# The last group of the second feed-forward product by eight block products, 128 tokens at a time, with its operands split during the seventh group

## The chip, the cores and the metric

The kernel runs on one core of one Trainium2 chip. The metric is the device time of one execution in microseconds, taken as the median of several runs. The core's engines are TensorE (PE in the profile), VectorE (DVE), ScalarE (ACT), GpSimd (POOL) and SyncE (SP), and DMA engines that move data beside them. Each of these engines works through its own list of instructions in the order in which the program issued them.

## The reference, cut to what matters

One decoder layer for 512 tokens of width 1024 in float32: a norm, three token mixers from one input projection, a gated merge, an output projection; then a feed-forward part and a final norm. The change touches only the feed-forward part's second product and the final norm behind it:

```python
h2 = rms_norm(x, g_ffn[l])
x = x + jnp.square(jax.nn.relu(h2 @ w_ff1[l])) @ w_ff2[l]
return rms_norm(x, g_final)
```

`w_ff1` is 1024x4096 and `w_ff2` 4096x1024. The hidden activation is therefore 512 tokens by 4096 columns.

## The kernel before, in words

**Split operands.** Each float32 operand of a matmul is split into a rounded part `hi` (a copy on ACT) and a rest `lo` (a subtraction on DVE that needs `hi`). One block of a product is three matmuls, hi by hi, hi by lo and lo by hi, in `mm3` (L96 to L100). In the feed-forward's second product the hidden activation is the stationary operand (128 columns of it, tokens) and 512 columns of the weight are streamed.

**Units and hooks.** The program is a list of units. A unit has a piece of matmul work and an eviction that is issued when the next unit begins. The main loop (L1082 to L1111) goes through the units. For unit i it issues, in this order: the `hi` copies of the weights due at slot i, the eviction of unit i-1, the `lo` subtractions of those weights, the hooks of slot i (table `pre`), a further weight load for each weight that was split, and then the matmuls of unit i. So what stands in the hooks of slot i goes to ACT, DVE and POOL while PE is in unit i-1 or at the start of unit i, and what it makes is for unit i or later.

**Two kinds of weight transfer.** Plain weight tiles come through SP into three `raw` buffers (L963) and are split at L971 (ACT) and L977 (DVE, shown as L79). A new load takes the buffer of the third load before it, so it waits for that one's `lo` subtraction. The second kind are block sums of `w_ff2`: POOL loads one 512 KB block (`w_load`, L748) and adds another to it by an accumulating transfer (`w_add`, L753); `w_split` (L757 to L762) splits the result into a ring of three `hi` and three `lo` buffers.

**The second product in groups of 512 hidden columns.** There are eight groups, g = 0 to 7. For one group the hidden tile is cut in 2x2 blocks (256 tokens by 256 hidden columns), the weight likewise (256 hidden columns by 512 outputs), and the 2x2 block product is done by seven block products of sums of blocks in place of eight of plain blocks. One such block product is 2 token tiles x 2 tiles of 128 hidden columns x 3 matmuls = 12 matmuls, so a group is 84. `form_11`, `form_12`, `form_22` split plain hidden blocks, `sum_3` and `sums` build sums of hidden blocks on DVE, and `form_s` splits these. The seven products are `stages` 1, 2, 5, 6, 3, 7, 4 (L778). `gather` (L773) adds each to the two or more quarters of the result `x2` that it belongs to; "B" is one accumulator that the products 1, 6, 7 and 4 add to in turn, and `gather` reads it between them.

**How groups overlap.** In the loop at L891, iteration g (1 to 7) has eight units: a tile of the first product of group g (24 matmuls, `f1_unit`, evicted by `ev_1`: DVE L691, ACT square L692), then products 1 and 2 of group g-1, a tile, products 5 and 6, a tile, products 3 and 7, a tile, product 4. The operands of the group's products are made in hooks during these. Iteration 8 (`last`) has no tiles of the first product left: seven units with one block product each, with its hooks (`sums`, `form_12`, three `w_split`, two `w_add`, `form_s` twice and more) squeezed into these seven slots.

**The end.** The final norm needs for each token the sum of squares over its 1024 outputs (`fin_sq`, ACT L807), a reciprocal root (`fin_rstd`: DVE, DVE L127, then a power on POOL) and a scaling by it and by the gain (`fin_dve` L822 on DVE, or `fin_gmul` and `fin_act` L827), and then the store. The table `ends` hangs these behind the products 2, 3 and 7 of the last group, and `fin_last` (L830) does the last two token tiles behind product 4.

Of the kernel before, what the change touches and what calls it, by code (L numbers as in the profile page):

```python
# [7 lines left out]
F32 = mybir.dt.float32  # L8
F32R = mybir.dt.float32r
# [27 lines left out]
def trunk_kernel(ctx: ExitStack, tc, xT, x_t, w_f, w_t, w_bc, w_a, w_o, w_1, w_2, vecs, rows, gfin, w_sg, cst, lmask, out):  # L37
# [31 lines left out]
    def hslot(i, dt):  # L69
        return rp.tile([P, 2 * S], dt, tag=f"h{i}", name=nm("h"))  # L70
# [31 lines left out]
    def cs(k, n=P):  # L102
        return slice(k * n, (k + 1) * n)
# [77 lines left out]
    def at(table, slot, fn, *a):  # L181
        table.setdefault(slot, []).append((fn, a))
# [561 lines left out]
    def w_tile(kind, dt):  # L744
        turns[kind] = turns[kind][1:] + turns[kind][:1]
        return zpair(turns[kind][-1], dt)

    def w_load(n, g, src, kind):  # L748
        if g < NG:
            wr[n, g] = w_tile(kind, F32)  # L750
            pool.dma_start(wr[n, g], w_2[g, src[0], src[1]])

    def w_add(n, g, src):  # L753
        if g < NG:
            pool.dma_start(wr[n, g], w_2[g, src[0], src[1]], accum_op=ALU.add)  # L755

    def w_split(n, src, g):  # L757
        if 0 <= g < NG:
            hi, lo = w_tile("h", F32R), w_tile("l", F32R)
            act.activation(hi, wr[src, g], AF.Copy)  # L760
            tt(dve, lo, wr[src, g], f(hi), ALU.subtract)
            wr[n, g, "r"] = (hi, lo)  # L762

    def product(g, a, b, key, start, stop):
        if start:
# [40 lines left out]
    def fin_sq(t, col):  # L806
        act.activation(tmp(), x2[t][:, cs(col, S)], AF.Square, accum_out=sf[col][:, t:t + 1])  # L807
# [22 lines left out]
    def fin_last():  # L830
        for j in range(2):
            t = 2 + j
            xv = x2[t][:, :S]
            tt(dve, xv, xv, part["B"][j], ALU.add)
            fin_sq(t, 0)
            fin_rstd(t, 1)
            fin_act(t, cs(1, S))
            fin_dve(t, cs(0, S))

    ends = {2: [(fin_sq, (0, 0)), (fin_sq, (1, 0))],  # L840
            3: [(fin_sq, (0, 1)), (fin_sq, (1, 1)), (fin_rstd, (0, 2))]
            + [(fin_dve, (t, cs(0, D))) for t in range(2)],
            7: [(fin_sq, (t, 1)) for t in (2, 3)] + [(fin_gmul, (t, 1, dve)) for t in (2, 3)]}

    o0 = len(units)
    for n in range(2):
        for j in range(4):
# [24 lines left out]

    W11, W12, W21, W22 = (0, 0), (0, 1), (1, 0), (1, 1)

    def chain(g):
        return f"c{g}"

    def early(u):

        at(pre, u, w_load, "c", 0, W12, "c")  # L880
# [7 lines left out]
    at(pre, f0 + 6, fin_gain)  # L888
    f1_unit(3)
    b0 = len(units)  # L890
    for g in range(1, NG + 1):  # L891
        u = len(units)
        last = g == NG
        h = g - 1
        if not last:
            order_ = [(4 * g, None), (None, (1, 2)), (4 * g + 1, None), (None, (5, 6)), (4 * g + 2, None), (None, (3, 7)),
                      (4 * g + 3, None), (None, (4,))]
            for i, ps in order_:
                if ps is None:
                    f1_unit(i, slot=len(units) - 1)  # L900
                else:
                    stage_unit(h, ps)
            sl = [u + x for x in range(8)]
        else:
# [10 lines left out]
        at(pre, sl[0], w_split, "21", "21", h)  # L915
# [15 lines left out]
        at(pre, sl[0], form_12)  # L931
        at(pre, sl[0], w_split, "t1", "c", h)
        at(pre, sl[0], w_add, "c", h, W22)
        at(pre, sl[0], form_s, "s12", 6)
        at(pre, sl[0], w_load, "22", h, W22, "p")
        at(pre, sl[1], form_s, "s34", 12)
        at(pre, sl[1], w_load, "11", g, W11, "p")
        at(pre, sl[2], w_split, "t3", "t3", h)
        at(pre, sl[2], w_split, "t2", "c", h)
        at(pre, sl[2], w_add, "c", h, W21)  # L940
        at(pre, sl[3], form_22)
        at(pre, sl[3], w_load, "t3", g, W12, "t3")
        at(pre, sl[4], w_split, "22", "22", h)
        at(pre, sl[4], sum_3)
        at(pre, sl[4], form_11)
        at(pre, sl[4], w_load, "c", g, W12, "c")
        at(pre, sl[5], w_split, "t4", "c", h)
        at(pre, sl[5], w_add, "t3", g, W22)
        at(pre, sl[5], w_load, "21", g, W21, "p")
        at(pre, sl[6], w_split, "11", "11", g)  # L950
        at(pre, sl[6], w_add, "c", g, W11)
        if g < NG - 1:
            at(pre, sl[7], sums)

    raws, ws = {}, {}
    order = [x for s in sorted(when) for x in when[s]]
# [210 lines left out]
```

## Time and profile before

| | |
|---|---|
| median of 3 runs | 850.81 us (849.37 to 851.62) |
| profiled execution: time, span | 851.69 us, 849.8 us |
| mean granted TensorE clock | 0.986 of full speed |
| PE busy | 823.8 us, 97% of the span |
| DVE, ACT, POOL busy | 65%, 41%, 19% |

The span runs from the first to the last instruction, and the execution's own time is 1.89 us above it. In a timeline a row is: start, duration, engine, line, operation, what it writes and reads, and in brackets how long the engine sat idle before it and what ended that. Matmul records overlap, since the engine is pipelined, so the step between starts, not the duration, is what one costs. A clock of 1.00 in a stretch is 2.4 GHz, one of 0.50 is 1.2 GHz.

### The profile page before, as it was taken

What the parts mean: (1) busy time and instruction counts of PE and PEld (TensorE: products, weight loads), DVE (VectorE), ACT (ScalarE), POOL (GpSimd) and SP (SyncE); (2) the same over time, 40 slices, a digit from 0 to 9 for tenths busy, and PEclk for the clock granted to TensorE, in tenths of its full rate; (3) what the DMA queues carried; (4) which work ended last, traced back from release to release, by engine and by line L of the source; (5) the groups of instructions that cost most, each with busy time, mean ns of one, the idle gap of its engine ahead of it and who ended that gap; (6) DMA issues with size and microseconds to landing.
All of it is one profiled execution on the core that took longest, in us unless ns stands there. A gap on an engine that the chain in (4) does not pass through costs nothing. (4 is left out here: it accounts for less than half of the span.)

```text
span 849.8 us, 9890 instructions
## 1 busy us (share of the span) xinstructions
PE 823.8 (97%) x3786; PEld 685.3 (81%) x3786; DVE 553.6 (65%) x720; ACT 350.9 (41%) x525; POOL 162.8 (19%) x193
## 2 busy tenths in 40 slices
PE   9999899999999999999999999999999999999973
PEld 7888688888888888888888888888888888888752
DVE  7556989978573445554444457595968686868574
ACT  7567355354333232232322445343435353534232
POOL 4313565661210000000000020102111111112000
PEclk9999999999999999999999999999999999999986
DMA  8321222212112323222234264837474656665432
GB/s 302 123 100 50 74 100 76 72 54 95 55 62 100 105 93 103 96 86 95 92 137 173 100 211 126 233 125 198 125 197 139 184 156 168 169 176 148 100 49 100
DMA packets 31296, 105.06 MB, mean 124 GB/s; under 512 B 3601, under 2 KB 3985, under 8 KB 31249
## 3 DMA queue, kind: packets, MB, share of 16 engines
q1 hardware_dynamic: 20448, 66.13, 21.9%
q0 software_dynamic: 10368, 37.75, 18.2%
q8 instruction: 29, 0.48, 0.2%
q10 hardware_dynamic: 432, 0.55, 0.2%
q14 instruction: 19, 0.15, 0.1%
HBM read 102.33 MB, written 2.10 MB: 123 GB/s over the span
## 5 line engine op out<-in xcount | busy, mean ns | idle before, releaser
L98 PE MATMUL acc<-x,wh 128*128 128x512 f32 x672 | 263.6, 392 | 0.0
L100 PE MATMUL acc<-x,wl 128*128 128x512 f32 x672 | 261.6, 389 | 0.0
L99 PE MATMUL acc<-x,wh 128*128 128x512 f32 x672 | 261.5, 389 | 0.0
L971 ACT ACTIVATE wh<-raw 128x1024 fp32r<-128x1024 f32 (+1 forms) x112 | 114.6, 1025 | 245.9 <-PE acc L99 143.5
L79 DVE TENSOR_TENSOR wl<-raw,wh 128x1024 fp32r<-128x1024 f32 (+1 forms) x118 | 150.1, 1273 | 43.9 <-ACT wh L971 43.8
L100 PEld LDWEIGHTS acc<-x,wl 128*128 128x128 f32 x672 | 126.1, 188 | 26.3
L98 PEld LDWEIGHTS acc<-x,wh 128*128 128x128 f32 x672 | 126.2, 188 | 25.9 <-issue 0.2
L99 PEld LDWEIGHTS acc<-x,wh 128*128 128x128 f32 x672 | 126.2, 188 | 25.6 <-issue 0.2
L79 DVE TENSOR_TENSOR z<-z,z 128x1024 fp32r<-128x1024 f32 x56 | 67.8, 1220 | 38.8 <-ACT z L760 38.8
L79 DVE TENSOR_TENSOR h<-h,acc 128x512 f32<-128x512 f32 x124 | 79.4, 682 | 11.0 <-PE acc L100 11.0
L98 PE MATMUL acc<-z,h 128*128 128x512 f32 x192 | 77.3, 403 | 7.8 <-DVE h L79 6.9
L760 ACT ACTIVATE z<-z 128x1024 fp32r<-128x1024 f32 x56 | 58.1, 1051 | 52.2 <-PE acc L100 28.1
L100 PE MATMUL acc<-z,h 128*128 128x512 f32 x192 | 77.0, 401 | 1.9 <-DVE h L79 1.9
L99 PE MATMUL acc<-z,h 128*128 128x512 f32 x192 | 77.1, 401 | 0.8 <-DVE z L79 0.8
L755 POOL DMA_DIRECT2D z<-w x32 | 28.1, 877 | 253.4 <-DVE z L79 208.4
L79 DVE TENSOR_TENSOR h<-h,h 128x256 f32<-128x256 f32 (+4 forms) x94 | 70.2, 752 | 7.0 <-ACT h L736 3.6
L692 ACT ACTIVATE h<-tmp 128x512 f32<-128x512 f32 x32 | 20.3, 633 | 126.9 <-DVE tmp L691 126.9
L79 DVE TENSOR_TENSOR tmp<-acc,rb 128x512 f32<-128x512 f32 x28 | 19.4, 691 | 79.0 <-PE acc L100 79.0
L79 POOL TENSOR_TENSOR tmp<-tmp,tmp 128x512 f32<-128x512 f32 x15 | 20.4, 1357 | 197.8 <-DVE tmp L79 185.0
L98 PEld LDWEIGHTS acc<-z,h 128*128 128x128 f32 x192 | 37.3, 194 | 16.8 <-issue 7.7
L100 PEld LDWEIGHTS acc<-z,h 128*128 128x128 f32 x192 | 37.5, 195 | 10.3 <-DVE h L79 2.4
L99 PEld LDWEIGHTS acc<-z,h 128*128 128x128 f32 x192 | 37.4, 195 | 8.9 <-DVE z L79 1.1
(186 smaller groups left out, 1045.3 us busy)
## 6 DMA issues: line engine op xcount, KB each, us to landing
z<-w POOLq DMA_DIRECT2D x72, 512.0 KB, 6.4
raw<-w_f SPq DMA_DIRECT2D x52, 512.0 KB, 3.2
raw<-w SPq DMA_DIRECT2D x32, 512.0 KB, 5.6
raw<-w_bc SPq DMA_DIRECT2D x8, 512.0 KB, 3.2
raw<-w_o SPq DMA_DIRECT2D x8, 512.0 KB, 3.2
raw<-w_t SPq DMA_DIRECT2D x4, 512.0 KB, 3.2
raw<-w_a SPq DMA_DIRECT2D x8, 256.0 KB, 2.6
h<-x_t SPq DMA_DIRECT2D x4, 512.0 KB, 7.5
```

What stands on the lines that cost most here:

```text
L79: return e.tensor_tensor(out=o, in0=a, in1=b, op=op)
L98: pe.matmul(o, lh, rh, start=start, stop=False, skip_group_check=more)
L99: pe.matmul(o, lh, rl, start=False, stop=False, skip_group_check=more)
L100: pe.matmul(o, ll, rh, start=False, stop=stop, skip_group_check=more)
L692: act.activation(hf["a" if r < 2 else "b"][:, cs(r % 2, S)], t, AF.Square)
L755: pool.dma_start(wr[n, g], w_2[g, src[0], src[1]], accum_op=ALU.add)
L760: act.activation(hi, wr[src, g], AF.Copy)
L971: act.activation(hi[:, :n], raws[i][:, :n], AF.Copy)
```

## The change

Groups 0 to 6 keep the seven products; iteration 7, which does group 6's products and the last four tiles of the first product, now also prepares group 7 in another way, and iteration 8 is gone. In its place stand five units: token tiles 0, 1 and 2 with both halves of the outputs, then tile 3 with the left half and tile 3 with the right half. Each half of a token tile is one accumulator of 4 blocks of 128 hidden columns x 3 = 12 matmuls, so the group is 96. All four `w_ff2` blocks of the group are used as they are: the two of the first 256 hidden columns come through SP and the `raw` buffers (`w2a`), the other two through POOL ("11" and "12", without sums). The hidden activation is split whole, by `full_split`: "a" (columns 0 to 255) at slot u+4, the two halves of "b" at u+6 and u+7. The evictions add each accumulator to `x2` once and run the final norm tile by tile; tile 3's left half is multiplied by the gain before its right half is done. The tables `ends`, `fin_last` and `chain` are removed, as are the tests for the group number in `w_load`, `w_add` and `w_split`; the lines for groups 1 to 6 are only moved. The diff, cut to its core:

```diff
+    def full_split(n, half):
+
+        if half == 0:
+            hr[n] = (hslot(6, F32R), hslot(7, F32R)) if n == "a" else (hslot(4, F32R), hslot(5, F32R))
+        c = slice(0, 2 * S) if n == "a" else cs(half, S)
+        hi, lo = hr[n]
+        act.activation(hi[:, c], hf[n][:, c], AF.Copy)
+        tt(dve, lo[:, c], hf[n][:, c], f(hi[:, c]), ALU.subtract)
...
-                if g == NG - 1:
-                    for fn, args in ends.get(p, []):
-                        fn(*args)
...
-    for g in range(1, NG + 1):
+    for g in range(1, NG):
         u = len(units)
-        last = g == NG
...
-        else:
-            for p in (1, 2, 5, 6, 3, 7):
-                stage_unit(h, (p,))
-            units.append((None, lambda w: stages[4](NG - 1), lambda a: fin_last()))
-            sl = [u - 1, u, u + 1, u + 1, u + 3, u + 4, u + 5, u + 6]
...
         if last:
-            at(pre, u, sums)
-            at(pre, u, w_load, "22", h, W22, "p")
-            at(pre, u, form_12)
-            at(pre, u, w_split, "t1", "c", h)
-            at(pre, u, w_add, "c", h, W22)
-            at(pre, u, form_s, "s12", 6)
-            at(pre, u + 1, form_s, "s34", 12)
-            at(pre, u + 1, w_split, "t2", "c", h)
-            at(pre, u + 1, w_add, "c", h, W21)
-            at(pre, u + 2, form_22)
-            at(pre, u + 2, w_split, "22", "22", h)
-            at(pre, u + 3, w_split, "t3", "t3", h)
+            at(pre, u + 3, w_load, "11", g, W21, "p")
+            at(pre, u + 4, w_load, "12", g, W22, "p")
+            at(pre, u + 4, full_split, "a", 0)
             at(pre, u + 5, w_split, "t4", "c", h)
-            continue
...
+            at(pre, u + 6, w_split, "11", "11", g)
+            at(pre, u + 6, full_split, "b", 0)
+            at(pre, u + 7, full_split, "b", 1)
+            at(pre, u + 7, w_split, "12", "12", g)
+            w2a = [load(u + 5, w_2[g, 0, 0]), load(u + 6, w_2[g, 0, 1])]
+        else:
...
+    def last_mm(t, ns):
+        def mm(w):
+            for n in ns:
+                a = part["l", n] = acc()
+                for b in range(4):
+                    hh, hl = hr["a" if b < 2 else "b"]
+                    wh_, wl2 = ws[w2a[n]] if b < 2 else wr["11" if n == 0 else "12", NG - 1, "r"]
+                    c = slice(b % 2 * S + t * P, b % 2 * S + (t + 1) * P)
+                    mm3(a, hh[:, c], hl[:, c], wh_[:, cs(b % 2, S)], wl2[:, cs(b % 2, S)], b == 0, b == 3)
+        return mm
+
+    def last_ev(t, ns):
+        for n in ns:
+            xv = x2[t][:, cs(n, S)]
+            tt(dve, xv, xv, part["l", n], ALU.add)
+            fin_sq(t, n)
+        if len(ns) == 1 and n == 0:
+            fin_gmul(t, 0, dve)
+        elif n == 1:
+            fin_rstd(t, 1)
+            if len(ns) == 2:
+                fin_dve(t, cs(0, D))
+            else:
+                fin_act(t, cs(0, S))
+                fin_dve(t, cs(1, S))
+
+    for t, ns in ((0, (0, 1)), (1, (0, 1)), (2, (0, 1)), (3, (0,)), (3, (1,))):
+        units.append((None, last_mm(t, ns), lambda a, t=t, ns=ns: last_ev(t, ns)))
```

## Rows read from the trace of the kernel before

**Rows 1.** The page's first part: busy time, share, instructions of each engine.
```profile
PE 823.8 (97%) x3786; PEld 685.3 (81%) x3786; DVE 553.6 (65%) x720; ACT 350.9 (41%) x525; POOL 162.8 (19%) x193
```
**Rows 2.** Windows: stretch, length, busy (records) PE PEld DVE ACT POOL, clock, DMA, GB/s.
```profile
780.00:800.00 20.00, 20.00 (x90) 16.57 (x89) 11.84 (x17) 5.90 (x8) 2.32 (x3) 1.00 0.64 152
...
803.12:840.00 36.88, 26.26 (x85) 19.22 (x83) 26.39 (x37) 13.01 (x25) 3.00 (x4) 0.82 0.28 69
...
809.50:812.50 3.00, 3.00 (x9) 2.34 (x7) 3.00 (x4) 0.00 (x0) 0.87 (x1) 0.50 0.44 51
...
834.40:840.00 5.60, 5.46 (x12) 3.77 (x12) 2.88 (x7) 2.06 (x7) 0.55 (x1) 0.50 0.05 20
```
**Rows 3.** Timeline of PE: iteration 7 from unit u+4, then the last group.
```profile
784.08 0.39 PE L98 MATMUL acc<-x,wh 128*128 128x512 f32 x1
...
789.30 0.39 PE L100 MATMUL acc<-x,wl 128*128 128x512 f32 x1
...
803.12 0.39 PE L98 MATMUL acc<-z,z 128*128 128x512 f32 x1
...
808.39 0.50 PE L100 MATMUL acc<-z,h 128*128 128x512 f32 x1 [1.93 <-DVE h L79]
...
816.10 0.50 PE L98 MATMUL acc<-z,h 128*128 128x512 f32 x1 [0.84 <-ACT z L760]
817.36 0.50 PE L99 MATMUL acc<-z,h 128*128 128x512 f32 x1 [0.76 <-DVE z L79]
...
822.75 0.58 PE L98 MATMUL acc<-z,h 128*128 128x512 f32 x1 [2.62 <-DVE h L79]
...
834.40 0.76 PE L98 MATMUL acc<-z,h 128*128 128x512 f32 x1 [4.32 <-DVE h L79]
...
839.23 0.63 PE L100 MATMUL acc<-z,h 128*128 128x512 f32 x1
```
**Rows 4.** Timeline of ACT: the seventh group's end and the last group.
```profile
795.16 2.01 ACT L760 ACTIVATE z<-z 128x1024 fp32r<-128x1024 f32 x2 [4.02 <-PE acc L100]
801.64 0.63 ACT L692 ACTIVATE h<-tmp 128x512 f32<-128x512 f32 x1 [4.47 <-DVE tmp L691]
...
814.99 1.06 ACT L760 ACTIVATE z<-z 128x1024 fp32r<-128x1024 f32 x1 [5.95 <-DMA z<-w]
```
**Rows 5.** Timeline of DVE: iteration 7 from unit u+2, and the end.
```profile
779.45 1.22 DVE L79 TENSOR_TENSOR wl<-raw,wh 128x1024 fp32r<-128x1024 f32 x1
...
784.89 1.22 DVE L79 TENSOR_TENSOR z<-z,z 128x1024 fp32r<-128x1024 f32 x1
...
789.72 0.69 DVE L691 SCALAR_TENSOR_TENSOR tmp<-acc,rb 128x512 f32<-128x512 f32 x1 [2.41 <-PE acc L100]
...
796.25 1.23 DVE L79 TENSOR_TENSOR z<-z,z 128x1024 fp32r<-128x1024 f32 x1 [4.71 <-ACT z L760]
797.40 2.47 DVE L79 TENSOR_TENSOR h<-h,acc 128x512 f32<-128x512 f32 x4
799.79 1.21 DVE L79 TENSOR_TENSOR z<-z,z 128x1024 fp32r<-128x1024 f32 x1
800.93 0.68 DVE L691 SCALAR_TENSOR_TENSOR tmp<-acc,rb 128x512 f32<-128x512 f32 x1
...
837.34 0.69 DVE L79 TENSOR_TENSOR h<-h,acc 128x512 f32<-128x512 f32 x1 [0.99 <-PE acc L100]
...
839.88 0.75 DVE L822 SCALAR_TENSOR_TENSOR h<-h,rr,h 128x512 f32<-128x512 f32 x1 [0.66 <-POOL rr L79]
840.55 0.68 DVE L79 TENSOR_TENSOR h<-h,acc 128x512 f32<-128x512 f32 x1
```
**Rows 6.** Timeline of POOL, one row; POOL's issues to `z` from 760 us, time to landing.
```profile
777.64 0.89 POOL L755 DMA_DIRECT2D z<-w  x1 [7.31 <-DVE z L79]
...
DMA to landing us min/median/max: 3.6/5.9/7.7
```
**Rows 7.** The tile `raw` from 740 us: time from SP's issue to landing.
```profile
DMA to landing us min/median/max: 3.3/5.5/7.1
```

More of the change, by code (lines that the diff above doesn't have):

```diff
@@ L748, in w_load @@
     def w_load(n, g, src, kind):
-        if g < NG:
-            wr[n, g] = w_tile(kind, F32)
-            pool.dma_start(wr[n, g], w_2[g, src[0], src[1]])
+        wr[n, g] = w_tile(kind, F32)
+        pool.dma_start(wr[n, g], w_2[g, src[0], src[1]])
     def w_add(n, g, src):
-        if g < NG:
-            pool.dma_start(wr[n, g], w_2[g, src[0], src[1]], accum_op=ALU.add)
+        pool.dma_start(wr[n, g], w_2[g, src[0], src[1]], accum_op=ALU.add)
     def w_split(n, src, g):
[L758 to L762, printed above, removed]
+        hi, lo = w_tile("h", F32R), w_tile("l", F32R)
+        act.activation(hi, wr[src, g], AF.Copy)
+        tt(dve, lo, wr[src, g], f(hi), ALU.subtract)
+        wr[n, g, "r"] = (hi, lo)
     def product(g, a, b, key, start, stop):
@@ L828, in fin_act @@
         nc.scalar.dma_start(out[t, :, c], xv)
[L830 to L843, printed above, removed]
     o0 = len(units)
@@ L873, in trunk_kernel @@
     W11, W12, W21, W22 = (0, 0), (0, 1), (1, 0), (1, 1)
-    def chain(g):
-        return f"c{g}"
     def early(u):
@@ L890, in trunk_kernel @@
     b0 = len(units)
-    for g in range(1, NG + 1):
+    for g in range(1, NG):
         u = len(units)
-        last = g == NG
         h = g - 1
[L895 to L900, printed above, removed]
-                else:
-                    stage_unit(h, ps)
-            sl = [u + x for x in range(8)]
-        else:
-            for p in (1, 2, 5, 6, 3, 7):
-                stage_unit(h, (p,))
-            units.append((None, lambda w: stages[4](NG - 1), lambda a: fin_last()))
-            sl = [u - 1, u, u + 1, u + 1, u + 3, u + 4, u + 5, u + 6]
+        last = g == NG - 1
+        for i, ps in ((0, None), (None, (1, 2)), (1, None), (None, (5, 6)), (2, None), (None, (3, 7)), (3, None), (None, (4,))):
+            if ps is None:
+                f1_unit(4 * g + i, slot=len(units) - 1)
+            else:
+                stage_unit(h, ps)
         if g == 1:
@@ L914, in trunk_kernel @@
             at(pre, u, sums)
-        at(pre, sl[0], w_split, "21", "21", h)
-        if last:
-            at(pre, u, sums)
-            at(pre, u, w_load, "22", h, W22, "p")
-            at(pre, u, form_12)
-            at(pre, u, w_split, "t1", "c", h)
-            at(pre, u, w_add, "c", h, W22)
-            at(pre, u, form_s, "s12", 6)
-            at(pre, u + 1, form_s, "s34", 12)
-            at(pre, u + 1, w_split, "t2", "c", h)
-            at(pre, u + 1, w_add, "c", h, W21)
-            at(pre, u + 2, form_22)
-            at(pre, u + 2, w_split, "22", "22", h)
-            at(pre, u + 3, w_split, "t3", "t3", h)
-            at(pre, u + 5, w_split, "t4", "c", h)
-            continue
@@ L931, in trunk_kernel @@
[L931 to L953, printed above, removed]
+        at(pre, u, w_split, "21", "21", h)
+        at(pre, u, form_12)
@@ new lines, in trunk_kernel @@
+        at(pre, u, w_split, "t1", "c", h)
+        at(pre, u, w_add, "c", h, W22)
+        at(pre, u, form_s, "s12", 6)
+        at(pre, u, w_load, "22", h, W22, "p")
+        at(pre, u + 1, form_s, "s34", 12)
+        at(pre, u + 2, w_split, "t3", "t3", h)
+        at(pre, u + 2, w_split, "t2", "c", h)
+        at(pre, u + 2, w_add, "c", h, W21)
+        at(pre, u + 3, form_22)
+        at(pre, u + 4, w_split, "22", "22", h)
+        if last:
+            at(pre, u + 3, w_load, "11", g, W21, "p")
+            at(pre, u + 4, w_load, "12", g, W22, "p")
+            at(pre, u + 4, full_split, "a", 0)
+            at(pre, u + 5, w_split, "t4", "c", h)
+            at(pre, u + 6, w_split, "11", "11", g)
[4 more added lines that the diff above has]
+        else:
+            at(pre, u + 1, w_load, "11", g, W11, "p")
+            at(pre, u + 3, w_load, "t3", g, W12, "t3")
+            at(pre, u + 4, sum_3)
+            at(pre, u + 4, form_11)
+            at(pre, u + 4, w_load, "c", g, W12, "c")
+            at(pre, u + 5, w_split, "t4", "c", h)
+            at(pre, u + 5, w_add, "t3", g, W22)
+            at(pre, u + 5, w_load, "21", g, W21, "p")
+            at(pre, u + 6, w_split, "11", "11", g)
+            at(pre, u + 6, w_add, "c", g, W11)
+            at(pre, u + 7, sums)
@@ new lines, in last_ev @@
+    def last_ev(t, ns):
[9 more added lines that the diff above has]
+                fin_dve(t, cs(0, D))
+            else:
+                fin_act(t, cs(0, S))
+                fin_dve(t, cs(1, S))
+    for t, ns in ((0, (0, 1)), (1, (0, 1)), (2, (0, 1)), (3, (0,)), (3, (1,))):
+        units.append((None, last_mm(t, ns), lambda a, t=t, ns=ns: last_ev(t, ns)))
```

## Prediction

> **What bounds the kernel now.** I read the page first: PE is busy for 97% of the span [rows 1], so almost everywhere time goes only where PE's work goes. Then the windows, to see where the other 3% lies. In iteration 7 PE is busy in all of 780 to 800 us at full clock [rows 2]; in the last group, 803.12 to 840.00, it is busy 26.26 of 36.88 us at a mean clock of 0.82 [rows 2]. So the last group is limited by something else, and the PE timeline shows by what: five waits, of 1.93, 0.84, 0.76, 2.62 and 4.32 us, ended by DVE or ACT where they finish a split operand [rows 3]. ACT's own wait before such a split is for a weight transfer: 5.95 us until the accumulating load landed [rows 4]. That is the chain: split a weight sum, only then add the next block into its buffer, only then split again. Beside the waits PE runs a part of the group at 1.2 GHz: 0.50 at 809.5 to 812.5 and at 834.4 to 840 [rows 2].
>
> The price of a matmul at full clock comes from iteration 7: from 784.08 to 803.12 [rows 3] there are 24 + 24 + 24 + 12 = 84, so one is 19.04 / 84 = 0.2267 us. The last group's first matmul starts at 803.12, its 84th at 839.23 [rows 3], 36.11 us later, where 83 steps of 0.2267 would be 18.82. **17.29 us** of it are waits and low clock.
>
> By the Trainium skill (TensorE: Matmul & The Clock Gate, Back-to-back issue gap) a 512-column matmul at the high clock costs 512/2.4 + 2.5 ns = 0.216 us, and by this estimate the 95 steps below would be 20.5 us and the result 834.7; the trace does not agree, with 0.2267 over 84 matmuls, and I stay with it.
>
> **The change, part by part.**
>
> 1. *Products.* 96 matmuls take the place of 84: 12 x 0.2267 = +2.72 us on PE.
>
> 2. *The waits of the last group.* They go if all operands are there in time: -17.29 us. POOL's two accumulating adds and one load vanish from the last group itself; in iteration 7 POOL issues two loads ("11", "12") where it had six further issues. Whether the operands are in time I follow queue by queue.
>
> SP: two more 512 KB loads, the last of its list before the stores. The second waits for the raw buffer of the third load before, free when DVE's subtraction of 779.45 ends at 780.7 [rows 5]; with the longest landing of 7.1 us [rows 7] it is there at 787.8, and its copy on ACT comes after 796 (below). The first is one place earlier. The stores are queued behind these loads on SP, but are issued 20 us later.
>
> POOL: "11" follows the add issued at 777.64 [rows 6] and needs no new buffer; with 0.89 for that issue and 7.7 us to landing [rows 6] it is there by 787. "12" takes the buffer of "22", free when DVE's subtraction of 784.89 ends at 786.1 [rows 5]: there by 794.7. Both are split after 796. Behind "12" nothing is queued on POOL until the final norm.
>
> ACT: `full_split` "a" needs the buffers of product 6's operands, whose evictions are awaited at that place anyway; it takes about 1.0 us in place of `form_11`. Then comes the copy of "t4", which waits for product 7's end: it starts at 795.16 [rows 4], and behind it wait the copies of w2a's second tile, "11" and the first half of "b". Two full copies take 2.01 [rows 4], so these three (the half one taken as 0.6) run from 796.2 to 798.8.
>
> DVE decides. In iteration 7 it gets six subtractions more, full ones for w2a twice, "12" and "a", halves for "b" twice, and loses `sum_3` and `form_11`, two halves that "a" outweighs exactly. A full one steps 1.14 (799.79 to 800.93), a half or an eviction 0.60 ((799.79 - 797.40) / 4) [rows 5]: net 3 x 1.14 + 2 x 0.60 = 4.6 us. The first of w2a lies in the 4.71 us of idle before 796.25 [rows 5]. The rest queues behind the four evictions that end at 799.79: w2a second tile to 800.93, "11" to 802.07, first half of "b" to 802.7. Now the last tile's eviction, at 800.93 before [rows 5], runs at 802.7 to 803.4; its square on ACT waits for it (0.63, [rows 4]): 804.0; the copy of the second half of "b" to 804.6, its subtraction to 805.3; the copy of "12" to 805.6, its subtraction to 806.8. The evictions of product 4 wait behind that to 808, and nobody waits for them soon.
>
> PE wants these from 803.12: blocks 0 and 1 at once (long there); block 2 ("11", first half of "b": 802.7) after 6 matmuls, at 804.48; block 3 at 805.16 (copy 804.6, and its third matmul, at 805.61, the subtraction of 805.3); the right half's blocks 0 and 1 at 805.84; block 2 at 807.20 ("12": 806.8). All are in time, with margins of 0.3 to 1.8 us. So I price the wait at **0**. No row shows this order of work; the nearest is the wait of 1.93 at 808.39 for the same kind of operand [rows 3], with low clock behind it: 3.00 us in the stretch from 809.5 for 7 steps of 0.427 where full clock needs 1.59 [rows 2], so 1.4 lost. Upper end: 1.93 + 1.4 = 3.3. Below nothing is excluded, since PE cannot begin before iteration 7's last product has left it at 803.12. I take 0, as the margins are worked out from rows of the very queues. After token tile 0 all operands are there.
>
> 3. *The end.* The last matmul then starts at 803.12 + 95 x 0.2267 = 824.66. DVE takes up an accumulator 0.42 after its last matmul's start (789.30 and 789.72, [rows 3, 5]): 825.08. But DVE may still be busy with tiles 2 and 3-left: tile 2's last accumulator is out at 803.12 + 71 x 0.2267 + 0.42 = 819.64; from such an eviction to the scaling are 839.88 - 837.34 = 2.54 [rows 5], the scaling of 1024 columns is 2 x 0.60 = 1.2: DVE free at 823.4; tile 3-left's eviction 0.6, its square on ACT 0.8, multiply 0.6: 825.4. So the last eviction starts at 825.4, **0.35** late. From there the chain (square, root, power, scaling, store from ACT and SP of 256 KB each) is the one that followed the eviction at 840.55 [rows 5]: 849.80 - 840.55 = 9.25. Before, that eviction came 1.32 after the last matmul's start (839.23), now 0.77: -0.55. The stores of tiles 0 to 2 are out well before; tile 2's is issued some 5 us ahead of the last.
>
> Final norm of tiles 0 to 2: per tile two evictions, two squares, root and scaling, 2.54 + 0.6 + 1.2 = 4.3 us of DVE, waits included, against PE's 24 x 0.2267 = 5.44: hidden. If it were not, each tile would put the end back by the difference.
>
> **Sum**: -17.29 + 2.72 - 0.55 = **-15.1 us**. Span 849.8 - 15.1 = 834.7, execution 851.69 - 15.1 = 836.6. The profiled execution is 0.88 above the median, so for the median 850.81 - 15.1 = **835.7**.
>
> **Rivals.**
>
> *A late operand in the first token tile.* DVE's chain slips by a microsecond, PE waits at block 3 or at "12", and the clock falls. For it: margins of 0.3 us, and this is just what happened at 808.39. Against: it needs a slip of the DVE queue that before held to its order. Price at the bound, 3.3: **839.0**.
>
> *The change doesn't do what it says*: the operands still come in a chain through the last group, and the 17 us of waits remain in other places. Then +2.7 and some relief: **about 851**. Against: no transfer of the new group waits for a split of the same group.
>
> *Slower: the clock.* The accumulator now closes every 12 matmuls throughout, and DVE works at every close. If PE were starved at each and the last group ran at 1.2 GHz, one step would be (839.23 - 834.40) / 11 = 0.44 [rows 3] and 96 would take 42.2 in place of 21.8: +20.4, so **856.1**. It decides where 15.1 / 0.21 = 71 of the 96 run at the low level. For it: 0.50 in two stretches of the old group [rows 2]. Against: each of these stands behind a wait, and from 780 to 800, where accumulators close after 12 or 24 too, the clock is 1.00 [rows 2].
>
> The Trainium skill (the same page, A second HAM failure mode: psum-queue depth-cycling) tells of a kernel whose clock swings where it goes through accumulators; the trace agrees only in the waits, not in 780 to 800.
>
> **How the numbers follow.** Forecast 0.71, its own range 834.5 to 838.0; late operand 0.21; no gain 0.04; slower 0.04. The range reaches from 834.0 (no DVE delay at the end, less the 1.3 us by which single runs of before differ) to 840.2 (the late operand, and as much above): it leaves out some 0.1. A measurement of this kernel tells apart about 0.3%, 2.6 us: faster 0.92, within 0.04, slower 0.04.
>
> **What the profile after would show.** Right: PE from about 803 without a wait, at clock 1.00 up to about 825, 96 steps of 0.2267; DVE's eviction of the last first-product tile some 1.8 us later than before; the last eviction about 9.3 us before the end; no accumulating POOL transfer after 778. Wrong: a wait of PE behind "12" or the second half of "b", a clock under 1.00 after 804, a wait of PE inside iteration 7 (a buffer that isn't free), or a last eviction that DVE reaches a microsecond or more late.

## The result and the profile after

The changed kernel takes **836.03 us** in the median of 4 runs (835.38 to 836.71), against 851.02 for the kernel before (4 runs, 849.37 to 851.62): a ratio of 0.9827, 95% interval 0.981 to 0.9844. The forecast was 835.7 for the median, 834.7 for the span and 836.6 for the profiled execution; measured were 836.03, 834.7 and 836.52.

The page's first part after, which answers to [rows 1]:

```profile
PE 819.6 (98%) x3798; PEld 683.8 (82%) x3798; DVE 542.2 (65%) x706; ACT 346.0 (41%) x519; POOL 155.6 (19%) x187
```

PE issues 12 instructions more (3798 against 3786) and is yet busy 4.2 us less; the windows show where. They are, columns as in [rows 2], 20 us of iteration 7, the last group from its first matmul on, and what follows.

```profile
780.00:800.00 20.00, 20.00 (x90) 16.57 (x89) 12.90 (x17) 9.28 (x11) 0.55 (x1) 1.00 0.33 103
...
803.69:825.50 21.81, 21.81 (x97) 17.82 (x95) 12.62 (x22) 7.28 (x17) 1.66 (x3) 1.00 0.15 61
...
825.00:835.00 10.00, 0.65 (x3) 0.19 (x1) 2.35 (x5) 1.87 (x5) 0.54 (x1) 0.64 0.25 100
```

In the last group PE is busy in all of 21.81 us at a clock of 1.00, where it was 26.26 of 36.88 at 0.82 [rows 2]. DVE has 12.62 us of work there in place of 26.39. Iteration 7 carries more than before (ACT 9.28 for 5.90 in its 20 us, DVE 12.90 for 11.84) and PE still has no idle time in it. The list of PE's waits from 700 us on is empty; before, it had the five of [rows 3]. PE's timeline: last group's first and last matmul.

```profile
803.69 0.39 PE L98 MATMUL acc<-wh,h 128*128 128x512 f32 x1
...
825.26 0.39 PE L100 MATMUL acc<-z,h 128*128 128x512 f32 x1
```

95 steps took 21.57 us, 0.2271 each. The timeline of DVE, which answers to [rows 5]: the last operands and the last evictions.

```profile
802.63 0.68 DVE L79 TENSOR_TENSOR h<-h,h 128x512 fp32r<-128x512 f32 x1
803.23 0.68 DVE L691 SCALAR_TENSOR_TENSOR tmp<-acc,rb 128x512 f32<-128x512 f32 x1
805.27 0.69 DVE L79 TENSOR_TENSOR h<-h,h 128x512 fp32r<-128x512 f32 x1 [1.36 <-ACT h L715]
806.23 1.23 DVE L79 TENSOR_TENSOR z<-z,z 128x1024 fp32r<-128x1024 f32 x1 [0.26 <-ACT z L766]
...
822.72 1.29 DVE L825 SCALAR_TENSOR_TENSOR h<-h,rr,h 128x1024 f32<-128x1024 f32 x1 [0.65 <-POOL rr L79]
823.92 0.68 DVE L79 TENSOR_TENSOR h<-h,acc 128x512 f32<-128x512 f32 x1
825.46 0.69 DVE L79 TENSOR_TENSOR h<-h,h 128x512 f32<-128x512 f32 x1 [0.85 <-ACT tmp L810]
826.06 0.68 DVE L79 TENSOR_TENSOR h<-h,acc 128x512 f32<-128x512 f32 x1
```

The first four rows are the order that the prediction worked out, each within 0.1 us of it once the 0.57 us by which this execution reached the last group later is taken off. The last four are the end: tile 2's scaling, tile 3's left eviction, its multiplication, then the last eviction at 826.06, 0.80 after the last matmul's start.

In what follows I compare executions from the first matmul of the last group to the end of the span, called **the last stretch**. It leaves out what differs ahead of that matmul, which started between 801.34 us (`e2_swap`) and 805.07 us (`e9_short`) in the executions below. The last stretch was 849.8 - 803.12 = 46.68 before and is 834.7 - 803.69 = 31.01 after, 15.67 less. Of this, 36.11 - 21.57 = 14.54 lie between the group's first and last matmul, where the waits and the low clock are gone, and 1.13 lie behind the last matmul's start (10.57 before, 9.44 after).

### The profile page after: what moved, and what is told of

It is laid out like the page before. It is cut to its first block, busy times and chain, and to the rows that moved or that the text cites. A ratio compares the mean times of both kernels' runs of the same rounds, so it can differ in the third digit from the quotient of the medians.

```text
span 834.7 us, 9871 instructions
## 1 busy us (share of the span) xinstructions
PE 819.6 (98%) x3798; PEld 683.8 (82%) x3798; DVE 542.2 (65%) x706; ACT 346.0 (41%) x519; POOL 155.6 (19%) x187
## 4 chain that ended last, share of the span: by engine, by line
PE 95%; DVE 2%; issue 2%; DMA 1%; ACT 0%; SPq 0%; POOLq 0%; POOL 0%; DVEq 0%
PE acc L98 29%; PE acc L99 29%; PE acc L100 29%; PE acc L326 3%; PE acc L1058 1%; DVE h L79 1%; DVE wl L79 1%; DMA raw<-w_t 1%; PE acc L478 0%; PE acc L379 0%; PE acc L641 0%; DVE h L307 0%; PE acc L381 0%; PE acc L362 0%; PE acc L402 0%
## 5 line engine op out<-in xcount | busy, mean ns | idle before, releaser
L972 ACT ACTIVATE wh<-raw 128x1024 fp32r<-128x1024 f32 (+1 forms) x114 | 116.6, 1025 | 246.7 <-PE acc L99 143.5
L79 DVE TENSOR_TENSOR wl<-raw,wh 128x1024 fp32r<-128x1024 f32 (+1 forms) x120 | 153.2, 1278 | 44.1 <-ACT wh L972 43.8
L79 DVE TENSOR_TENSOR h<-h,acc 128x512 f32<-128x512 f32 x118 | 75.6, 681 | 11.1 <-PE acc L100 11.0
L79 DVE TENSOR_TENSOR z<-z,z 128x1024 fp32r<-128x1024 f32 x51 | 61.6, 1218 | 32.1 <-ACT z L766 32.1
L766 ACT ACTIVATE z<-z 128x1024 fp32r<-128x1024 f32 x51 | 53.1, 1051 | 45.0 <-PE acc L100 28.2
L99 PE MATMUL acc<-z,h 128*128 128x512 f32 x184 | 71.6, 389 | 0.0
L100 PE MATMUL acc<-z,h 128*128 128x512 f32 x184 | 71.6, 389 | 0.0
L98 PE MATMUL acc<-z,h 128*128 128x512 f32 x184 | 71.6, 389 | 0.0
L79 DVE TENSOR_TENSOR h<-h,h 128x256 f32<-128x256 f32 (+4 forms) x89 | 66.4, 750 | 7.6 <-ACT h L745 3.6
L762 POOL DMA_DIRECT2D z<-w x28 | 24.5, 873 | 231.7 <-DVE z L79 195.6
L691 DVE SCALAR_TENSOR_TENSOR tmp<-acc,rb 128x512 f32<-128x512 f32 x32 | 22.0, 686 | 30.9 <-PE acc L100 30.9
L100 PEld LDWEIGHTS acc<-z,h 128*128 128x128 f32 x184 | 34.5, 188 | 7.3
L98 PEld LDWEIGHTS acc<-z,h 128*128 128x128 f32 x184 | 34.5, 188 | 7.2
```

Of the source, the lines that this page charges most:

```text
L98: pe.matmul(o, lh, rh, start=start, stop=False, skip_group_check=more)
L99: pe.matmul(o, lh, rl, start=False, stop=False, skip_group_check=more)
L100: pe.matmul(o, ll, rh, start=False, stop=stop, skip_group_check=more)
L691: dve.scalar_tensor_tensor(out=t, in0=part["f", i], scalar=0.0, in1=part["r2b"], op0=ALU.max, op1=ALU.mult)
L972: act.activation(hi[:, :n], raws[i][:, :n], AF.Copy)
```

## The experiments

### Were the operands needed early? Splits undone, and one pair exchanged

`e1_late_split`, on the changed kernel:

```diff
-            at(pre, u + 4, full_split, "a", 0)
...
-            at(pre, u + 6, w_split, "11", "11", g)
-            at(pre, u + 6, full_split, "b", 0)
-            at(pre, u + 7, full_split, "b", 1)
-            at(pre, u + 7, w_split, "12", "12", g)
+            at(pre, u + 8, full_split, "a", 0)
+            at(pre, u + 8, w_split, "11", "11", g)
+            at(pre, u + 8, full_split, "b", 0)
+            at(pre, u + 8, full_split, "b", 1)
+            at(pre, u + 8, w_split, "12", "12", g)
```

> The changed kernel with one part undone: the splits of the hidden activation and of the two POOL weight blocks of the last group stand at the first slot of the last group and no longer in the seventh; products, order and loads are as in the changed kernel. Theory (the gain hangs on operands that are ready when PE gets to the last group): the subtraction for a, about 1.1 us, begins on DVE only behind product 4's evictions, so PE waits at the third matmul of the last group, in sum some 2 to 2.5 us in the first token tile, and runs at 1.2 GHz for a while behind it, up to 1.4 us: about 839 to 840 us. Rival (eight plain products without weight sums do it by themselves, where their operands are split does not matter): 836.0 within 0.5 us and no wait of PE.

Measured: 837.68 us, ratio to the kernel before 0.9837 (0.9817 to 0.9857). The last stretch is 836.0 - 802.96 = 33.04, 2.03 more than in the changed kernel. PE's timeline and the window around it:

```profile
802.96 0.50 PE L98 MATMUL acc<-wh,h 128*128 128x512 f32 x1
803.29 0.40 PE L99 MATMUL acc<-wl,h 128*128 128x512 f32 x1
804.88 0.50 PE L100 MATMUL acc<-wh,h 128*128 128x512 f32 x1 [1.19 <-DVE h L79]
```
```profile
803.00:807.00 4.00, 2.73 (x10) 1.64 (x11) 4.00 (x5) 2.84 (x4) 0.00 (x0) 1.00 0.00 0
```

The wait is where it was expected, at the third matmul, ended by DVE. DVE was busy for all 4.00 us. The clock stayed at 1.00, so the 1.4 us for low clock did not come, and the time is below the 839 to 840 that was expected.

`e2_swap`, on the changed kernel:

```diff
-            at(pre, u + 7, full_split, "b", 1)
             at(pre, u + 7, w_split, "12", "12", g)
+            at(pre, u + 7, full_split, "b", 1)
```

> The changed kernel with two hooks of slot u+7 exchanged: the split of weight block 12 ahead of the second half of b. It puts the second half of b about 1.1 us later on ACT and DVE. Theory (margins of 0.3 to 0.7 us at block 3, worked out from the queues, are real and no more): PE waits at block 3 for the copy (about 0.5 us) and the subtraction (about 0.7 us more), 1.2 us in sum, and loses up to 1.4 us more if the granted clock falls to 0.5 behind it: 837.2 to 838.6 us. Rival (there is slack that the rows did not show): no wait, 836.0 us. Rival of the clock: a single wait of 1 us is enough to bring the low clock, then the profile shows under 1.00 for a stretch behind 806.

Measured: 837.15 us, ratio 0.9832 (0.9814 to 0.9851). PE's timeline at block 3:

```profile
803.16 0.39 PE L100 MATMUL acc<-z,h 128*128 128x512 f32 x1
803.75 0.50 PE L98 MATMUL acc<-z,h 128*128 128x512 f32 x1 [0.21 <-ACT h L715]
804.10 0.39 PE L99 MATMUL acc<-z,h 128*128 128x512 f32 x1
805.10 0.50 PE L100 MATMUL acc<-z,h 128*128 128x512 f32 x1 [0.61 <-DVE h L79]
```

Both waits came at the two matmuls named. Between starts there are 0.59, 0.35 and 1.00 us where three steps would be 0.68: 1.26 lost, with 0.82 shown in the brackets. The last stretch, 833.8 - 801.34 = 32.46, is 1.45 longer. So the margins were as thin as worked out, and again the clock stayed at 1.00 (the windows up to 820 show nothing else).

### Is PE alone the pace now? Token order, and 12 matmuls fewer

`e3_halves`, on the changed kernel:

```diff
-    for t, ns in ((0, (0, 1)), (1, (0, 1)), (2, (0, 1)), (3, (0,)), (3, (1,))):
+    for t, ns in [(t, (n,)) for n in range(2) for t in range(4)]:
```

> The changed kernel with the last group's ten half tiles in another order: the left output halves of token tiles 0 to 3, then the right halves of tiles 0 to 3, each with its own final norm. Same products and operands. Theory (the end is set by DVE's chain behind the last eviction, and a tile's norm costs DVE 3.2 us against 2.72 us of PE per half tile): DVE falls behind by 0.5 us with each right half, so the last eviction starts 1.4 to 1.8 us after PE has it ready instead of 0.4: 837.0 to 837.6 us, PE without a wait. Rival (the token order has no part in the gain, the final norm is hidden either way): 836.0 us within 0.4 us.

Measured: 836.74 us, ratio 0.9833 (0.9816 to 0.9851), which the timing cannot tell from the changed kernel. (The expectation's "ten half tiles" are eight.) The trace can: the last stretch is 836.4 - 804.46 = 31.94, 0.93 more. PE ends as it should, DVE does not:

```profile
825.99 0.39 PE L100 MATMUL acc<-z,h 128*128 128x512 f32 x1
```
```profile
824.60 0.68 DVE L79 TENSOR_TENSOR h<-h,acc 128x512 f32<-128x512 f32 x1
...
827.07 0.75 DVE L825 SCALAR_TENSOR_TENSOR h<-h,rr,h 128x512 f32<-128x512 f32 x1 [0.65 <-POOL rr L79]
827.74 0.68 DVE L79 TENSOR_TENSOR h<-h,acc 128x512 f32<-128x512 f32 x1
```

A tile's norm takes DVE 827.74 - 824.60 = 3.14 us against 2.72 of PE. The last eviction starts 1.75 after the last matmul's start instead of 0.80. Going tile by tile is worth about 0.9 us of the gain.

`e4_fewer`, on the changed kernel:

```diff
+                    if b == 2 or (b == 1 and n == 0):
+                        pe.matmul(a, hh[:, c], wh_[:, cs(b % 2, S)], start=False, stop=False)
+                        pe.matmul(a, hh[:, c], wl2[:, cs(b % 2, S)], start=False, stop=False)
+                        continue
```

> The changed kernel with 12 of the last group's 96 matmuls left out (the part lo by hi of some blocks of every token tile, so that part of the product is not computed): 84 as in the group before. Theory (PE alone sets the pace of the last group now, each matmul 0.2267 us): 2.7 us less, 833.3 us, still without a wait of PE. Rival (another engine's chain is as long): less than 1.5 us gained, and DVE or ACT show no more idle time.

Measured: 834.71 us, ratio 0.9805 (0.9783 to 0.9827). By the medians this is 1.3 us less than the changed kernel, and the last stretch is 832.4 - 802.98 = 29.42, 1.59 less, not 2.72. PE's part shrank by 21.57 - (822.23 - 802.98) = 2.32. The rest of the 12 steps went to small delays in the first token tile, since fewer matmuls reach block 3 sooner. And 0.69 came back at the end:

```profile
820.38 1.28 DVE L825 SCALAR_TENSOR_TENSOR h<-h,rr,h 128x1024 f32<-128x1024 f32 x1 [0.65 <-POOL rr L79]
821.58 0.68 DVE L79 TENSOR_TENSOR h<-h,acc 128x512 f32<-128x512 f32 x1
823.11 0.69 DVE L79 TENSOR_TENSOR h<-h,h 128x512 f32<-128x512 f32 x1 [0.85 <-ACT tmp L810]
823.72 0.68 DVE L79 TENSOR_TENSOR h<-h,acc 128x512 f32<-128x512 f32 x1
```

The last eviction starts 823.72 - 822.23 = 1.49 after the last matmul's start, because DVE is still at tiles 2 and 3. So the theory for this run was too simple, and its rival is half right: PE sets the pace in the changed kernel, but DVE's norm is right behind it, though DVE still has idle time in its rows.

### What bounded the old last group?

The prediction named the chain of split, accumulating transfer and split. Three edits of the kernel before each relieve one suspected part: one leaves out the transfers, one moves the norm, one keeps PE at work during its waits.

`e5_no_add`:

```diff
             at(pre, u, w_split, "t1", "c", h)
-            at(pre, u, w_add, "c", h, W22)
...
-            at(pre, u + 1, w_add, "c", h, W21)
```

> The kernel before with the two accumulating transfers of the last group left out (two of its weight sums are then not formed, so two block products are computed with other weights). Theory of the prediction (the chain of split, add, split through one weight buffer is what bounded the old last group): the waits of PE before product 6 (1.6 us) go and those before products 3 and 4 shrink too, together 5 us or more: 846 us or less. Rival (the transfers ended only the waits before product 6; the others are ended by DVE's own queue): 1 to 2.5 us less, 848.5 to 850 us, the wait of over 4 us before product 4 stays.

`e8_order`:

```diff
-            3: [(fin_sq, (0, 1)), (fin_sq, (1, 1)), (fin_rstd, (0, 2))]
-            + [(fin_dve, (t, cs(0, D))) for t in range(2)],
-            7: [(fin_sq, (t, 1)) for t in (2, 3)] + [(fin_gmul, (t, 1, dve)) for t in (2, 3)]}
+            3: [(fin_sq, (0, 1)), (fin_sq, (1, 1))],
+            7: [(fin_rstd, (0, 2))] + [(fin_dve, (t, cs(0, D))) for t in range(2)] + [(fin_sq, (t, 1)) for t in (2, 3)] + [(fin_gmul, (t, 1, dve)) for t in (2, 3)]}
```

> The kernel before with one step moved: root and scaling of token tiles 0 and 1 go behind product 7's evictions, so that the subtraction for the last weight operand t4 no longer stands behind them on DVE. Rival to the theory of the prediction (the longest wait, 4.3 us before product 4, was DVE's queue and not the weight transfer): that wait shrinks to 1 us or less and the low clock behind it goes at least in part, 3 to 5 us in sum, but the two scalings then stand later in front of the last evictions and take back up to 2 us: 846 to 849 us. Theory (the transfer chain): the wait before product 4 stays above 3 us and the time at 851 within 1 us.

`e6_fill`, where `filled(p, k)` issues k matmuls of a finished operand into a spare accumulator ahead of product p:

```diff
-            for p in (1, 2, 5, 6, 3, 7):
...
+            for p, k in ((1, 0), (2, 9), (5, 0), (6, 8), (3, 12), (7, 0)):
                 stage_unit(h, (p,))
-            units.append((None, lambda w: stages[4](NG - 1), lambda a: fin_last()))
+                units[-1] = (None, filled(p, k), units[-1][2])
+            units.append((None, filled(4, 19), lambda a: fin_last()))
```

> The kernel before with 48 extra matmuls of 512 columns, whose result nobody reads, in the places where PE waited in the last group (9, 8, 12 and 19, each set about as long as its wait at 0.2267 us). It keeps PE at work and takes nothing away. Theory (of the 17.29 us that the old group took beyond its 84 steps some 11.4 are waits and 5.9 low clock, but the clock in the middle only shifts time into the next wait): the granted clock stays at 1.00, and only what lies behind the last wait gains, 12 matmuls by 0.2 us, 2 to 3 us: 848 to 849 us. Rival (the low clock costs its whole 5.9 us): 845 us. Rival (the fill is too long and delays the real products): 851 us or more.

Measured, each against 850.6 us: `e5_no_add` 847.92 (ratio 0.9971, 0.9961 to 0.9981), `e8_order` 850.64 (1.0, 0.9989 to 1.001), `e6_fill` 849.04 (0.9981, 0.9969 to 0.9993). PE's waits in the last group, without the transfers (us in total, how often, the longest):

```profile
PE acc L98 <- DVE h L79: 6.9, 2, 4.3
PE acc L100 <- DVE h L79: 1.9, 1, 1.9
PE acc L99 <- DVE z L79: 0.2, 1, 0.2
```

Without them the wait on ACT goes, the one on `z` shrinks to 0.2, and the three others stay as they were, the longest of 4.3 among them. So the transfers ended only the waits at product 6; they are worth 2.7 us by the medians and 2.5 by the ratio (847.3 - 804.08 = 43.22, 3.46 less, in the last stretch of one execution), and the prediction's chain explains no more than that.

What the longest wait was for stands in DVE's timeline of the kernel before:

```profile
830.04 2.48 DVE L822 SCALAR_TENSOR_TENSOR h<-h,rr,h 128x1024 f32<-128x1024 f32 x2 [0.83 <-POOL rr L79]
832.44 1.22 DVE L79 TENSOR_TENSOR z<-z,z 128x1024 fp32r<-128x1024 f32 x1
833.57 1.28 DVE L79 TENSOR_TENSOR h<-h,acc 128x512 f32<-128x512 f32 x2
```

Product 4 adds to the accumulators "B" that product 7 left, and starts at 834.40 [rows 3], right behind the first of the two evictions of 833.57. Product 7's last matmul had started at 829.69; its evictions stood behind the norm of tiles 0 and 1 and behind t4's subtraction. The wait of 2.62 before product 3 is of the same kind: it ends behind product 5's eviction. With the norm moved (`e8_order`) the wait before product 4 falls from 4.32 to 1.71 and the low clock behind it goes:

```profile
831.76 0.47 PE L98 MATMUL acc<-z,h 128*128 128x512 f32 x1 [1.71 <-DVE h L79]
834.37 0.39 PE L100 MATMUL acc<-z,h 128*128 128x512 f32 x1
```
```profile
833.31 2.48 DVE L822 SCALAR_TENSOR_TENSOR h<-h,rr,h 128x1024 f32<-128x1024 f32 x2 [0.83 <-POOL rr L79]
835.71 1.28 DVE L79 TENSOR_TENSOR h<-h,h 128x512 f32<-128x512 f32 x2
836.92 0.68 DVE L79 TENSOR_TENSOR h<-h,acc 128x512 f32<-128x512 f32 x1
```

PE is done 4.9 us earlier (834.37 for 839.23), and the time does not move: the scalings now stand in front of the last evictions. Neither expectation is met as a whole: the wait shrank, though not to 1 us, and the time stayed where the transfer theory had it, for another reason. The longest wait was DVE's queue, and behind PE the same queue held the end.

The fill shows the clock's share. The stretch that had 0.50 before [rows 2], and the first and last matmul of product 4:

```profile
809.50:812.50 3.00, 3.00 (x15) 2.48 (x14) 3.00 (x5) 0.00 (x0) 0.87 (x1) 1.00 0.40 49
```
```profile
833.19 0.47 PE L98 MATMUL acc<-z,h 128*128 128x512 f32 x1 [0.19 <-DVE h L79]
...
835.80 0.39 PE L100 MATMUL acc<-z,h 128*128 128x512 f32 x1
```

With a clock of 1.00 all through the group the gain is 1.6 us in the median and 46.68 - (847.5 - 803.21) = 2.39 in the last stretch, far from 5.9. That is about what the 12 matmuls behind the last wait were expected to give, but in part by luck. From first to last matmul the group is 36.11 - (835.80 - 803.21) = 3.52 shorter, 2.2 of it in those 12 matmuls and 1.3 ahead of them, where product 3 ran at 1.00 (from 823 to 827 us the kernel before had 0.58). So the low clock in the middle did not only move time into the next wait. Behind the last matmul 1.13 came back, in DVE's queue.

Three more versions follow from this.

`e10_pool`, on the kernel before, with scaling by the root on ACT and by the gain on POOL:

```diff
+    def fin_pool(t):
+        act.activation(x2[t], x2[t], AF.Copy, scale=part["fr", t])
+        tt(pool, x2[t], x2[t], part["gf"], ALU.mult)
+        nc.sync.dma_start(out[t], x2[t])
...
-            + [(fin_dve, (t, cs(0, D))) for t in range(2)],
+            + [(fin_pool, (t,)) for t in range(2)],
```

> The kernel before with the final scaling of token tiles 0 and 1 taken off DVE: ACT multiplies by the root, POOL by the gain, in place of two DVE passes of 1.2 us each in front of the subtraction for t4 and of the last evictions. Theory now (the work in DVE's one queue is what bounded the old last group): t4's subtraction starts some 2.4 us earlier, product 4 finds the clock at 1.00, and nothing comes back later on DVE: the last eviction 3 to 4.5 us earlier, 846 to 847.5 us. Rival (the accumulating transfers bound it): less than 1 us gained.

`e11_pool_noadd` is this edit and that of `e5_no_add` together.

> The kernel before with both relieved: scaling of tiles 0 and 1 off DVE as in the run beside it, and the last group's two accumulating transfers left out (so two block products are computed with other weights). Theory (DVE's queue and the transfers are two separate shares, and even without both the seven products need sums of the hidden tile that exist only after its last eviction): the shares add, 2.5 to 3 us for the transfers and 3 to 4.5 us for DVE, 843 to 845.5 us, some 7 us above the changed kernel, with the waits at product 2 and before product 3 still there. Rival (either one hides the other): within 1 us of the better of the two alone. Rival (these two were all that held the old group): 838 us or less.

`e12_weave`, on the kernel before:

```diff
             fin_sq(t, 0)
+            fin_dve(j, cs(0, D))
             fin_rstd(t, 1)
...
-            3: [(fin_sq, (0, 1)), (fin_sq, (1, 1)), (fin_rstd, (0, 2))]
-            + [(fin_dve, (t, cs(0, D))) for t in range(2)],
-            7: [(fin_sq, (t, 1)) for t in (2, 3)] + [(fin_gmul, (t, 1, dve)) for t in (2, 3)]}
+            3: [(fin_sq, (0, 1)), (fin_sq, (1, 1))],
+            7: [(fin_rstd, (0, 2))] + [(fin_sq, (t, 1)) for t in (2, 3)] + [(fin_gmul, (t, 1, dve)) for t in (2, 3)]}
```

> The kernel before with the final norm of token tiles 0 and 1 taken out of the way on both engines: its root goes behind product 7's evictions, and its two DVE scalings into the gaps in which DVE waits for the squares and roots of tiles 2 and 3. No work is left out and no transfer touched. Theory now (the norm standing in the in-order queues of DVE and ACT ahead of t4's split and of the last evictions made the old group's longest wait and its late end): product 4 waits 2 us or less, the clock behind it is 1.00, the end comes 2 to 3 us earlier, 848 to 849 us, and no more, since the waits at products 2, 6 and 3 stay. Rival (the transfers set the end): within 0.8 us of the kernel before. Rival (all of the old group's loss was this order): 840 us or less.

Measured: `e10_pool` 852.22 (ratio 1.0014, 1.0004 to 1.0023), `e11_pool_noadd` 849.72 (0.9976, 0.9963 to 0.9989), `e12_weave` 848.39 (0.9969, 0.9957 to 0.9981). In `e10_pool` the theory failed, the time is 1.2 us longer by the ratio. ACT's timeline and DVE's:

```profile
828.69 2.19 ACT L831 ACTIVATE h<-h,rr 128x1024 f32<-128x1024 f32 x2 [1.23 <-POOL rr L79]
830.78 1.04 ACT L760 ACTIVATE z<-z 128x1024 fp32r<-128x1024 f32 x1
```
```profile
831.86 1.49 DVE L79 TENSOR_TENSOR z<-z,z 128x1024 fp32r<-128x1024 f32 x1 [4.00 <-ACT z L760]
...
834.74 1.99 DVE L79 TENSOR_TENSOR h<-h,h 128x512 f32<-128x512 f32 x2 [0.19 <-ACT tmp L807]
```

The two scalings now stand on ACT ahead of t4's copy, and DVE waits 4.00 us for that copy. So it was not DVE's 2.4 us of work alone but the norm's place ahead of t4's split, with its wait for squares and root, that made the longest wait; moved to ACT's queue it costs as much. `e12_weave` takes it out of the way on both and gains what was expected: 2.6 us by the ratio (0.0031 x 850.5), the last stretch 847.1 - 803.30 = 43.80, 2.88 less. Its product 4:

```profile
832.26 0.47 PE L98 MATMUL acc<-z,h 128*128 128x512 f32 x1 [1.69 <-DVE h L79]
...
834.87 0.39 PE L100 MATMUL acc<-z,h 128*128 128x512 f32 x1
```

`e11_pool_noadd` came out 4 us above what was expected, since it carries the loss of `e10_pool`; but against that run the transfers are worth 852.22 - 849.72 = 2.5 us, as they are alone. The two shares do not hide each other there. Whether they add with the order of `e12_weave` was not tried.

No version of the seven products came under 847.9 us. In `e12_weave` the waits at product 2 (1.93), 6 (1.15 and 0.76), 3 (2.60) and 4 (1.69) stay. The one at product 2 is ended by the split of a hidden block behind the three sums, which exist only after the last tile's eviction; the changed kernel has no such sums in its last group, and no accumulator there has to be read between two products, as "B" and "C" have before products 4 and 3. How the rest of the 15.67 us divides beyond the shares of these runs is not shown, and a last group of seven products with all waits removed was not tried.

### Versions of the changed kernel

`e7_defer`: DVE takes tile 2's scaling behind tile 3's left eviction.

```diff
+            fin_dve(2, cs(0, D))
             fin_gmul(t, 0, dve)
...
-            if len(ns) == 2:
+            if t < 2:
                 fin_dve(t, cs(0, D))
-            else:
+            elif t == 3:
```

> The changed kernel with the scaling of token tile 2 moved behind the eviction and square of tile 3's left half, so that DVE is free when the last accumulator is ready. Theory (the last eviction starts 0.35 to 0.4 us late because DVE still scales tile 2): the last eviction follows the last matmul's start by 0.42 instead of 0.80 us, 835.6 us in the median, which a measurement can hardly tell from 836.0. Rival (the order moves the wait to the store of tile 2): the end stays or gets later by up to 0.5 us.

Measured: 835.58 us, ratio 0.9824 (0.9804 to 0.9843). DVE's last evictions, behind a last matmul that starts at 824.70:

```profile
823.01 1.28 DVE L825 SCALAR_TENSOR_TENSOR h<-h,rr,h 128x1024 f32<-128x1024 f32 x1
824.21 0.68 DVE L79 TENSOR_TENSOR h<-h,h 128x512 f32<-128x512 f32 x1
825.12 0.69 DVE L79 TENSOR_TENSOR h<-h,acc 128x512 f32<-128x512 f32 x1 [0.23 <-PE acc L100]
```

DVE now waits for PE, and the eviction follows by 0.42 as expected. The last stretch is 833.8 - 803.11 = 30.69, 0.32 less.

`e9_short` adds to it a fused sum ahead of the root:

```diff
-        tt(dve, q[:, :n], sf[0][:, t:t + n], sf[1][:, t:t + n], ALU.add)
-        rsqrt_cols(q[:, :n], n, 1.0 / D, EPS, r)
+        dve.scalar_tensor_tensor(out=q[:, :n], in0=sf[0][:, t:t + n], scalar=EPS, in1=sf[1][:, t:t + n], op0=ALU.add, op1=ALU.add)
+        tt(pool, r[:, :n], q[:, :n], mhalf[:, :n], ALU.pow)
```

(with `scale=1.0 / 32` in `fin_sq`, so that the squares add up to the mean)

> The changed kernel with tile 2's scaling moved behind tile 3's left eviction, as in the run that tried this alone, and one small DVE operation fewer between the last square and the power (the mean's factor is put into the square, the eps into the addition). Theory: from the last eviction's start to the span's end 0.2 us less than 8.66, together with the other 0.4 some 0.55 us under the changed kernel, 835.4 us in the median; in the trace plain, in the median hardly. Rival: the small operation was hidden beside POOL's start, nothing changes at the end.

Measured: 835.66 us, ratio 0.9822 (0.9807 to 0.9837). The last stretch is 835.5 - 805.07 = 30.43, 0.58 less than in the changed kernel, as worked out. By the medians neither version can be told from the changed kernel; the traces say that each is a little shorter at the end.

## Why the prediction was right, and where it was not

*Products.* Right in what they cost PE: 95 steps, 21.57 us, where 95 x 0.2267 = 21.54 was forecast.

*The waits go.* Right: none is left, and the operands came in the order and at the times worked out. `e1_late_split` shows that their place in the seventh group carries some 2 us of it, `e2_swap` that the margins are real.

*The chain named as the bound.* This reading failed, without harm to the sum. Of the five waits "ended by DVE or ACT where they finish a split operand" two were ended by evictions, the two longest. "Split a weight sum, only then add the next block into its buffer, only then split again" was taken from one wait of ACT for a transfer [rows 4]; `e5_no_add` gives it some 2.7 of the 15 us. The longest was the final norm, ahead of t4's split and product 7's evictions in the engines' own queues (`e8_order`, `e10_pool`, `e12_weave`). The sum did not need the chain: it took all of 17.29 us away because the new group has none of these steps ahead of its operands.

*A late operand.* The rival did not come. Its price of 3.3 us was too high for such a wait: 1.4 to 2.0 in the two runs that forced one. The low clock that was part of it did not follow.

*The end.* The last eviction came 0.80 after the last matmul's start (0.77 forecast, where the prediction's own terms add up to 0.72). From it to the span's end were 834.7 - 826.06 = 8.64 us, where the term was 9.25: mis-sized by 0.61. The operations up to ACT's last store take 3.29 where they took 3.24, as ACT's rows after and before show:

```profile
829.35 0.37 ACTq L831 DMA_DIRECT2D out<-h  x1
```
```profile
843.79 0.37 ACTq L828 DMA_DIRECT2D out<-h  x1
```

So the difference lies behind that issue; what it is no row shows. From the last eviction to the end it is 8.64 to 8.73 in the changed kernel and its versions, and 9.03 to 9.25 in the kernel before and its versions (without `e9_short` and `e12_weave`, where other work stands there), so it goes with the kernel and not with the execution.

*The start.* In this execution the last group began 0.57 later than before, in code that is not changed. It cancels the 0.61; that the forecast of the span met to 0.1 us is therefore luck, its terms being good to about 0.6.

*Slower.* No sign of it: the clock stayed at 1.00 though the accumulators close every 12 matmuls. The Trainium skill (TensorE: Matmul & The Clock Gate, A second HAM failure mode: psum-queue depth-cycling) puts such swings of the clock down to short idle times of PE between groups of matmuls. PE had none here, so this run neither bears that out nor speaks against it.

## What to carry to other kernels

A cheaper algorithm is only cheaper where its preparation is hidden: at the last step of a pipeline, with no work left to cover sums and splits, the plain form with 12 matmuls more was 15 us faster than the clever one, and still 13 us faster where its splits were not done ahead (`e1_late_split`). To forecast such a change, follow each in-order queue with durations from neighbouring rows, and compare each operand's time with the matmul that wants it; if all margins hold, price the stage by the bounding engine's step alone. And do not name a bound from the one wait that looks plain: the bracket of a row says which instruction came last; whether it was a split or an eviction, and what stood ahead of it in its queue, has to be looked up.

## What the runs showed of the hardware that was not expected

The same wait of 1.93 us at product 2 was followed by a clock of 0.50 in some executions and of 1.00 in others. The stretch 809.5 to 812.5 of `e10_pool` reads as below; the kernel before had 0.50 there [rows 2], `e8_order` and `e12_weave` 0.51, `e5_no_add` and `e11_pool_noadd` 1.00. A price for low clock behind a wait of this length is a bound, not a value.

```profile
809.50:812.50 3.00, 3.00 (x15) 2.45 (x14) 3.00 (x4) 0.00 (x0) 0.79 (x1) 1.00 0.54 60
```

A wait costs PE more than its row's bracket says: in `e2_swap` 1.26 us between starts for 0.82 shown, since records of 0.39 overlap in steps of 0.23 and the step behind a wait is 0.34.

DVE was slower beside POOL. In `e10_pool`, while POOL multiplied two tiles (first row, POOL's timeline), a 128x1024 subtraction took 1.49 us in place of 1.22, and two 128x512 products that began in that time 1.99 in place of 1.31 (second row, the kernel before). The evictions between them, which read an accumulator, took 1.27, where they took 1.28 before. `e11_pool_noadd` shows the same 1.49 and 1.99.

```profile
829.91 5.67 POOL L79 TENSOR_TENSOR h<-h,h 128x1024 f32<-128x1024 f32 x2 [1.26 <-ACT h L831]
```
```profile
835.04 1.31 DVE L79 TENSOR_TENSOR h<-h,h 128x512 f32<-128x512 f32 x2 [0.19 <-ACT tmp L807]
```
